# Gate matrices of a mixture of experts in one transfer each, with buffers of their own

## The chip, the core and the metric

One core of a Trainium2 chip runs the whole decoder block in one launch. The metric is the device time of one execution in microseconds. The engines that matter here are TensorE (PE in the profile), VectorE (DVE), ScalarE (ACT), GpSimd (POOL) and SyncE (SP), which computes nothing and issues nearly all transfers, in the order of its program. The core's 16 DMA engines carry them.

## The reference

Sequence 512, width 1024, everything in float32, one layer:

```
h    = rmsnorm(x) ;  proj = h @ w_in                     # pool input, q, k, v, two gates
x    = x + (gate_p * (pool(u) @ w_pool_up) + gate_a * (diff_attention(q, k, v) @ w_attn_up)) @ w_out
hn   = rmsnorm(x)
g    = top-1 of 4 expert groups(hn) ;  e1, e2 = top-2 of the 8 experts in that group
y[t] = sum over e in (e1, e2) of  weight(t, e) * ( (silu(hn[t] @ w_gate[e]) * (hn[t] @ w_up[e])) @ w_down[e] )
out  = x + y
```

There are 32 experts. `w_gate[e]` and `w_up[e]` are 1024 x 512, `w_down[e]` is 512 x 1024: 2 MB each, 192 MB (MiB) in all, and every one is read from HBM in every execution, whichever experts the tokens choose.

## The kernel before

**First part, up to the output projection (some 315 us).** The matrices of the mixer come in 24 pieces of 1 MB (`pieces`). A piece is staged (`stage_to`), then split chunk by chunk by ACT and DVE into a high and a low part in float32r (`split_to`, lines 156 to 160), and PE makes three products for one (`tok_unit`, `ch_unit`). `tick()` stands behind each unit of 12 matmuls and puts the splits of pieces that come later, and other small tasks, between the units. `ch_group(19, ...)` is the last product group ahead of the output projection. Its evacuation (`evac_attn(1)`, lines 562 to 566) makes the second half of the merged branches, `mh` and `ml`. `out_proj()` then multiplies with `w_out`, adds the residual (`acc`), norms, ranks the tokens by expert, and stores the normed rows to DRAM on POOL's queue (`store_rows`), from where later pairs fetch theirs.

**Second part, the experts, two at a time (16 pairs).** A pair has 64 token slots for each of its two experts. Pair p runs in this order on PE: gate product, up product, the rest of the scatter of pair p - 1, transposes of the hidden values (`ht`) and of the next pair's rows (`spread`), down product in two halves (`y`, `half_down`), the scatter of the first half. In the down product, the first half of the columns already uses all four down pieces.

**Buffers.** All large tiles come from one pool of 23 buffers of 8 KB a partition (`S`): x, staged and split pieces, h (two pairs of high and low), attention's o and pooling's y (a pair each), gates, the residual and the normed rows, and then the weights of the experts. A new tile takes the buffer that was given back first; its first writer waits until the old tile's last reader is through. The DMA engines are handed a transfer when SP's wait is over, and whatever SP issues later stands behind it.

**Order of the weights.** `order` lists the pieces of all experts, pair by pair: four of the gates (two halves of two experts, 1 MB each), four of up, four of down. `prefetch(n)` issues the next n of them (line 620). In `out_proj` it is called with 8, 4, 3, 3 and 1; in pair p with 4 behind the gate product, 4 behind the up product (5 for p = 0) and 4 behind the down product. The last pair has smaller pieces: eight of up of 512 KB, two of down of 1 MB, four of down of 512 KB. At the end of `out_proj` one buffer `io` holds x of the current pair in its first half and the rows fetched for the next in its second.

Of the kernel before, what the change touches and what calls it, by code (L numbers as in the profile page):

```python
# [32 lines left out]
NEG = -1.0e30  # L33
W_SCALE = 2.0 ** 14

NBIG = 23
NSM = 8
WARM = 12
LEAD = 6
OUT_ORDER = ((0, 0), (1, 0), (0, 1), (2, 0), (1, 1), (3, 0), (2, 1), (3, 1))  # L40
STG = 2
PF = (8, 4, 3, 3)
PAIR_ORDER = (("g", (0, 1)), ("u", (0, 1)), ("d", (0, 1)))
LAST_ORDER = (("g", (0, 1)), ("v", (0, 1, 2, 3)), ("h", (0,)), ("q", (2, 3)))
PIECE = {"g": (4, 512), "u": (4, 512), "v": (2, 512), "d": (2, 1024), "h": (4, 512), "q": (4, 256)}


@with_exitstack
def hybrid_block_kernel(
# [33 lines left out]
    const = ctx.enter_context(tc.tile_pool(name="const", bufs=1))  # L83
    tiny = ctx.enter_context(tc.tile_pool(name="tiny", bufs=3))
    big = ctx.enter_context(tc.tile_pool(name="big", bufs=NBIG))
    sm = ctx.enter_context(tc.tile_pool(name="sm", bufs=NSM))
    dram = ctx.enter_context(tc.tile_pool(name="dram", bufs=1, space=bass.MemoryType.DRAM))
    psum = ctx.enter_context(tc.tile_pool(name="psum", bufs=8, space=bass.MemoryType.PSUM))
# [3 lines left out]

    def S(shape, dt=F32, name="s"):
        return big.tile(shape, dt, tag="S", name=f"{name}{next(names)}")

    def T(name="t"):
        return sm.tile([128, 512], F32, tag="T", name=f"{name}{next(names)}")
# [4 lines left out]
    def bank(name="b", shape=(128, 512)):  # L102
        return psum.tile(list(shape), F32, tag="B", name=f"{name}{next(names)}")
# [134 lines left out]
        stt(neglam, lsum[:, 1:2], -LAM_INIT, lsum[:, 0:1], op0=OP.add, op1=OP.subtract)  # L238


    hT = [(S([128, 4, SEQ], F32R, name="hTh"), S([128, 4, SEQ], F32R, name="hTl")) for _ in range(2)]
    rst = const.tile([128, NT], F32, name="rst")

    def h_norm(t):
# [70 lines left out]
    def attention():  # L315
# [73 lines left out]

        def o_transpose(i):  # L390
            if i == 0:
                oT.extend((S([128, H, SEQ], F32R, name="oTh"), S([128, H, SEQ], F32R, name="oTl")))
            on = st.pop(("on", i))
            b = bank("to", (128, H, 128))
            for h in range(H):
                nc.tensor.transpose(b[:, h, :], on[:, h * 128:(h + 1) * 128], ident)
            s = slice(i * 128, (i + 1) * 128)
            nc.scalar.mul(oT[0][:, :, s], b, cols[:, 4:5])
            stt(oT[1][:, :, s], b, cols[:, 4:5], f(oT[0][:, :, s]), op0=OP.mult, op1=OP.subtract)
# [20 lines left out]
    def pool_group(g, b):  # L420
        w = POOL_W[g]
        PAD = 16
        z = S([128, 3, PAD + SEQ], name="u")
        nc.gpsimd.memset(z[:, :, :PAD], 0.0)
        u = z[:, 0]
        nc.scalar.copy(u[:, PAD:], b)
        cur, k = 0, 1
        while k < w:
            nxt = 2 if cur == 1 else 1
            nc.gpsimd.tensor_tensor(z[:, nxt, PAD:], z[:, cur, PAD:], z[:, cur, PAD - k:PAD + SEQ - k], op=OP.add)  # L430
            cur, k = nxt, 2 * k
        yield
        s, d = z[:, cur], z[:, 3 - cur, :SEQ]
        stt(d[:, w:SEQ], s[:, PAD + w:], 1.0 / w, u[:, PAD + w:], op0=OP.mult, op1=OP.subtract)
        tt(d[:, :w], s[:, PAD:PAD + w], rc[:, :w], op=OP.mult)
        tt(d[:, :w], d[:, :w], u[:, PAD:PAD + w], op=OP.subtract)
        if g == 0:
            yT.extend((S([128, 4, SEQ], F32R, name="yTh"), S([128, 4, SEQ], F32R, name="yTl")))
        yield
        p = bank("y")  # L440
        mm(p, wgrp[:, g, :], d, start=True, stop=True)
        nc.scalar.mul(yT[0][:, g, :], p, cols[:, g:g + 1])
        stt(yT[1][:, g, :], p, cols[:, g:g + 1], f(yT[0][:, g, :]), op0=OP.mult, op1=OP.subtract)
        yield
# [151 lines left out]
    for e in range(0, NE, 2):  # L596
        for w, parts in LAST_ORDER if e == NE - 2 else PAIR_ORDER:
            for part in parts:
                for par in range(2):
                    order.append((w, e + par, part))  # L600
    e_next = [0]

    def expert_ap(w, e, half):
        e = ds(e, 1) if isinstance(e, int) else e
        if w in "hq":
            n = PIECE[w][1]
            return w_down[e].rearrange("e (p j) n -> p (e j) n", j=4)[:, :, n * half:n * (half + 1)]
        if w == "d":
            return w_down[e].rearrange("e (p j) n -> p (e j) n", j=4)[:, 2 * half:2 * half + 2, :]
        src = w_gate if w == "g" else w_up  # L610
        n = PIECE[w][0]
        return src[e].rearrange("e (p j) n -> p (e j) n", j=8)[:, n * half:n * (half + 1), :]

    def prefetch(n):
        for _ in range(n):
            if e_next[0] < len(order):
                key = order[e_next[0]]
                e_next[0] += 1
                st = S([128, *PIECE[key[0]]], name="e")
                nc.sync.dma_start(st, expert_ap(*key))  # L620
                ew[key] = st
# [21 lines left out]
    tok_row = const.tile([128, SEQ], F32, name="tok_row")  # L643
    nc.gpsimd.iota(tok_row, pattern=[[-1, SEQ]], base=SEQ, channel_multiplier=0, allow_small_or_imprecise_dtypes=True)
    sel = {}
    first = {}

    def x2_half(t, hf, b):
        a = acc_t(t)[:, hf * 512:(hf + 1) * 512]
# [127 lines left out]
    def out_proj():  # L777
        i = N_GEMM
        bs = [bank("wo") for _ in range(NT)]
        prefetch(PF[0])  # L780
        for kq in range(2):
            for t in range(NT):
                tok_unit(bs[t], i + kq, kq, t, merged, kq == 0, kq == 1)
                if kq == 1:
                    x2_half(t, 0, bs[t])
                    after(2, lambda t=t: rt_transpose(t, 0))
                tick()
        prefetch(PF[1])
        last = NT - 1
        bs = {}  # L790
        mid = {}
        for n, (t, kq) in enumerate(OUT_ORDER):
            if kq == 0:
                bs[t] = bank("wo")
            tok_unit(bs[t], i + 2 + kq, kq, t, merged, kq == 0, kq == 1, mid)
            mid = {}
            if kq == 1:
                x2_half(t, 1, bs[t])
                if t == last:
                    rt_select(last - 1, 5)  # L800
                x2_rstd(t)
                if t < last - 1:
                    mid = {1: lambda t=t: rt_transpose(t, 1)}
                    after(2, lambda t=t: norm2(t))
                    after(2, lambda t=t: store_rows(t))
                    after(2, lambda t=t: rt_logits(t, 0, 1))
                    after(2, lambda t=t: rt_select(t))
                    after(3, lambda t=t: ranked(t))
                elif t < last:
                    mid = {0: lambda t=t: rt_transpose(t, 1), 1: lambda t=t: rt_logits(t, 0),  # L810
                           2: lambda t=t: (norm2(t), rt_logits(t, 1), rt_select(t, 3))}
            tick()
        prefetch(PF[2])
        assert not tasks, tasks
        rt_logits(last, 0)
        rt_transpose(last, 1)
        gather_first(0, (0,))
        rt_logits(last, 1)
        rt_select(last - 1)
        ranked(last - 1)  # L820
        norm2(last)
        store_rows(last - 1)
        gather_first(0, (1,))
        gather_first(1)
        rt_select(last)
        prefetch(PF[3])
        first["io"] = S([128, 2, D], name="io")
        gather_first(last - 1)
        ranked(last)
        gather_first(last)  # L830
        store_rows(last)
        prefetch(1)
        pairs[0] = first
        for t in range(NT):
            rt_weights(t)
# [17 lines left out]
            first["x"] = x_of(first["b"])  # L853

    def x_of(bs):
        xT = first["io"][:, 0, :].rearrange("p (j s) -> p j s", j=ND)
        for i, b in enumerate(bs):
            jj = slice(i * 4, (i + 1) * 4)
            tt(xT[:, jj, :], b, g2p[:, jj, None].to_broadcast([128, 4, 128]), op=OP.mult)  # L859
        return xT  # L860
# [7 lines left out]
                                     bounds_check=SEQ - 1, oob_is_err=False)  # L868

    def fetch(p):  # L870
        rows = first["io"][:, 1, :]
        nc.gpsimd.memset(rows, 0.0)  # L872
        fetch_rows(rows, info[p][2])
        pairs[p]["rows"] = rows

# [34 lines left out]
    def ffn_in(b, xs, w, part):  # L910
        n = w[0].shape[1]
        for k in range(n):
            j = part * n + k
            for par in range(len(xs)):
                s = slice(par * CAP, (par + 1) * CAP)
                mm(b[s, :], xs[par][:, j, :], w[par][:, k, :], start=j == 0, stop=j == 7)  # L916
# [67 lines left out]
    def take(w, e, part):  # L984
        return [ew.pop((w, e + par, part)) for par in range(2)]
# [45 lines left out]
    def run_overflow():  # L1031
# [15 lines left out]
        with tc.For_i(0, n_over, 1) as i:  # L1047
# [16 lines left out]
            ts(wv[:CAP, 2:3], wv[:CAP, 0:1], wv[:CAP, 1:2], 1.0 / W_SCALE, op0=OP.add, op1=OP.mult)  # L1064
            for k, b in (("g", banks[3]), ("u", banks[4])):
                for half in range(2):
                    nc.sync.dma_start(w, expert_ap(k, ds(e, 1), half))
                    ffn_in(b, [xT], [w], half)
            nc.scalar.activation(sg[:CAP], banks[3][:CAP], AF.Silu)
            tt(h[:CAP], banks[4][:CAP].rearrange("p (q j) -> p j q", j=4),  # L1070
# [16 lines left out]
    for p in range(n_pair):  # L1087
# [5 lines left out]
            if q < n_pair:  # L1093
                prepare(q)
        bg_ = bank("gate")
        for half in range(2):
            ffn_in(bg_, xs, take("g", e, half), half)
        prefetch(4)
        bu = bank("up")
        for part in LAST_ORDER[1][1] if last_pair else range(2):  # L1100
            ffn_in(bu, xs, take("v" if last_pair else "u", e, part), part)
        prefetch(5 if p == 0 else 4)
        h = ffn_h(bg_, bu, 128)
        adds = [scatter_mms(*prev, t) for t in range(3)] if prev else []
        for q in (0, 1, 2) if p == 0 else (p + 2,):
# [75 lines left out]
```

## Time and profile before

| | |
|---|---|
| median of 3 runs | 800.28 us (798.57 to 801.16) |
| the profiled execution: its time | 800.73 us |
| its span | 798.9 us |
| PE busy | 771.1 us (97%) |
| DVE busy | 361.1 us (45%) |
| ACT busy | 204.0 us (26%) |
| queue of SP and its share of 16 DMA engines | 233.37 MB, 72.5% |
| chain that ended last | PE 70%, DMA 21%, DVE 5% |

All times in views are counted from the start of the span. A busy PE is not PE at its peak: a group of matmuls that waits for data between single matmuls can show as busy. "Idle before" of an engine, and the releaser behind it, say what an engine waited for; for SP's queue the same view lists what its transfers waited for before they were issued.

### The profile page before, as it was taken

The page shows a single profiled execution, that of the slowest core. Times are in us where ns is not written, and L with a number is a line of the kernel's source. Part 1 is how long each engine was busy: PE and PEld are TensorE (multiplying, and loading weights), DVE is VectorE, ACT ScalarE, POOL GpSimd, SP SyncE. Part 2 cuts the span into 40 slices and gives each one's busy share as a digit, 9 for nine tenths or more (in the row PEclk, how much of TensorE's full clock was granted, in tenths as well). Part 3 has the DMA queues.
Part 4 walks back from the last instruction along what each step waited for, and adds up shares of the span by engine and source line. Part 5 has one row for each costly group of instructions (what it writes and reads, how often), then busy time and mean ns, then how long its engine had stood idle before and what let it go on. Part 6 is the DMA issues. An engine that isn't in the chain of part 4 may idle for free.

```text
span 798.9 us, 9648 instructions
## 1 busy us (share of the span) xinstructions
PE 771.1 (97%) x3686; PEld 450.6 (56%) x3686; DVE 361.1 (45%) x848; ACT 204.0 (26%) x390; POOL 69.2 (9%) x85
## 2 busy tenths in 40 slices
PE   7999999999999999999999999999999999999995
PEld 6888777778888888733444344434444333334343
DVE  5644476545464733662536353335343423324233
ACT  5644445554533433420010001000100000001000
POOL 1131060000100001100010000000000000000000
PEclk9999999999999999989999999999999999999998
DMA  9621013113228782989999999999999999999994
GB/s 326 201 81 53 6 48 106 54 53 106 72 89 313 293 340 91 373 353 425 425 427 427 426 426 426 427 425 426 425 427 426 425 427 425 426 427 426 426 397 146
DMA packets 55711, 240.07 MB, mean 301 GB/s; under 512 B 11176, under 2 KB 14760, under 8 KB 32112
## 3 DMA queue, kind: packets, MB, share of 16 engines
q1 hardware_dynamic: 52928, 233.37, 72.5%
q0 software_dynamic: 2736, 6.07, 1.9%
q8 instruction: 30, 0.49, 0.2%
q14 instruction: 17, 0.14, 0.0%
HBM read 239.13 MB, written 4.19 MB: 305 GB/s over the span
## 4 chain that ended last, share of the span: by engine, by line
PE 70%; DMA 21%; DVE 5%; ACT 2%; issue 1%; SPq 0%; POOL 0%; DVEq 0%; ACTq 0%
PE y L965 9%; PE gate L916 8%; PE up L916 8%; DMA e<-in_w_expert_up_dram 8%; DMA e<-in_w_expert_down_dram 7%; PE g L282 6%; PE g L283 6%; PE g L284 6%; DMA e<-in_w_expert_gate_dram 5%; PE sc L977 5%; PE wo L271 2%; PE wo L273 2%; PE wo L272 2%; PE qk L325 1%; PE o L370 1%; PE v L271 1%
## 5 line engine op out<-in xcount | busy, mean ns | idle before, releaser
L916 PE MATMUL up<-e,io 128*64 128x512 f32 x512 | 119.4, 594 | 9.6 <-DMA e<-in_w_expert_up_dram 9.5
L916 PE MATMUL gate<-e,io 128*64 128x512 f32 x512 | 115.4, 596 | 1.7 <-DVE io L859 1.7
L965 PE MATMUL y<-e,hT 128*64 128x512 f32 x480 | 114.1, 605 | 0.7 <-ACT hT L931 0.7
L922 DVE TENSOR_TENSOR h<-up,sg 128x512 f32<-128x512 f32 x16 | 17.2, 1075 | 183.0 <-PE up L916 183.0
L916 PEld LDWEIGHTS up<-e,io 128*64 128x64 f32 x512 | 38.2, 137 | 87.1 <-issue 67.3
L916 PEld LDWEIGHTS gate<-e,io 128*64 128x64 f32 x512 | 37.9, 137 | 69.6 <-issue 60.0
L981 DVE TENSOR_TENSOR acc<-sc,acc 128x512 f32<-128x512 f32 x124 | 76.8, 683 | 0.2
L965 PEld LDWEIGHTS y<-e,hT 128*64 128x64 f32 x480 | 35.4, 139 | 69.0 <-issue 62.8
L157 DVE SCALAR_TENSOR_TENSOR wl<-w,g1c,wh 128x512 fp32r<-128x512 f32 x64 | 49.0, 792 | 38.6 <-ACT wh L156 38.5
L282 PE MATMUL g<-hTh,wh 128*128 128x512 f32 x160 | 64.8, 405 | 0.1
L283 PE MATMUL g<-hTl,wh 128*128 128x512 f32 x160 | 62.4, 390 | 0.0
L284 PE MATMUL g<-hTh,wl 128*128 128x512 f32 x160 | 62.4, 390 | 0.0
L971 DVE SCALAR_TENSOR_TENSOR yl<-y,wv,yh 128x512 fp32r<-128x512 f32 x31 | 23.3, 751 | 76.1 <-ACT yh L970 76.1
L977 PE MATMUL sc<-yh,PT 128*128 128x512 f32 x124 | 53.3, 430 | 0.0
L970 ACT ACTIVATE yh<-y,wv 128x512 fp32r<-128x512 f32 x31 | 21.3, 688 | 118.0 <-PE y L965 113.8
L977 PE MATMUL sc<-yl,PT 128*128 128x512 f32 x124 | 48.9, 394 | 0.0
L931 ACT COPY hT<-ht 128x512 f32<-128x512 f32 x16 | 9.4, 587 | 145.7 <-PE ht L929 145.7
L156 ACT ACTIVATE wh<-w,g1c 128x512 fp32r<-128x512 f32 x64 | 44.6, 720 | 0.9 <-DMA w<-in_w_in_dram 0.9
L872 POOL MEMSET io<- 128x1024 f32 x15 | 14.3, 952 | 335.7 <-PE xg L882 335.7
L920 ACT ACTIVATE sg<-gate 128x512 f32<-128x512 f32 x16 | 9.6, 597 | 130.5 <-PE gate L916 130.5
L977 PEld LDWEIGHTS sc<-yh,PT 128*128 128x128 f32 x124 | 23.3, 188 | 28.1 <-issue 24.7
L282 PEld LDWEIGHTS g<-hTh,wh 128*128 128x128 f32 x160 | 30.0, 188 | 13.1 <-issue 5.4
(227 smaller groups left out, 1089.3 us busy)
## 6 DMA issues: line engine op xcount, KB each, us to landing
e<-in_w_expert_gate_dram SPq DMA_DIRECT2D x64, 1024.0 KB, 19.7
e<-in_w_expert_down_dram SPq DMA_DIRECT2D x62, 1024.0 KB, 19.6
e<-in_w_expert_up_dram SPq DMA_DIRECT2D x60, 1024.0 KB, 20.2
w<-in_w_in_dram SPq DMA_DIRECT2D x16, 1024.0 KB, 5.6
w<-in_w_out_dram SPq DMA_DIRECT2D x4, 1024.0 KB, 6.0
e<-in_w_expert_up_dram SPq DMA_DIRECT2D x8, 512.0 KB, 14.1
x<-in_x_dram SPq DMA_DIRECT2D x4, 512.0 KB, 6.2
w<-in_w_pool_up_dram SPq DMA_DIRECT2D x2, 1024.0 KB, 4.9
```

The costliest lines, as they stand in the source:

```text
L156: nc.scalar.mul(hi, src, g)
L157: stt(lo, src, g, f(hi), op0=OP.mult, op1=OP.subtract)
L271: mm(b, ahi[:, k, s], whi[:, k, :], start=first and k == 0, stop=False)
L282: mm(b, whi[:, k, s], ahi[:, k, :], start=first and k == 0, stop=False)
L283: mm(b, whi[:, k, s], alo[:, k, :], start=False, stop=False)
L284: mm(b, wlo[:, k, s], ahi[:, k, :], start=False, stop=last and k == 3)
L916: mm(b[s, :], xs[par][:, j, :], w[par][:, k, :], start=j == 0, stop=j == 7)
L965: mm(y[r, :], hTt[:, j, r], w[j // 2][par][:, j % 2, hf * 512:(hf + 1) * 512], start=j == 0, stop=j == 3)
L970: nc.scalar.mul(hi, y, wv)
L971: stt(lo, y, wv, f(hi), op0=OP.mult, op1=OP.subtract)
L977: mm(b, PT[:, t * 128:(t + 1) * 128], y2[k], start=k == 0, stop=k == 1)
L981: tt(a, b, a, op=OP.add)
```

## The change

The pool of 23 buffers becomes one of 15 single ones and one of four of double size (16 KB a partition), the same memory. The four hold h (two), y of the pooling and o of attention first, and from the output projection on the gate matrices: one transfer of 2 MB for an expert's whole gate matrix. The list `order` holds up and down only; the gates have an iterator of their own, and `prefetch_gate()` issues the two of a pair. x and the fetched rows get a buffer each, of two halves that take turns; the buffer of the rows is asked for behind the last store of normed rows.

```diff
-NBIG = 23
+NBIG = 15
+NWIDE = 4
-PF = (8, 4, 3, 3)
-PAIR_ORDER = (("g", (0, 1)), ("u", (0, 1)), ("d", (0, 1)))
-LAST_ORDER = (("g", (0, 1)), ("v", (0, 1, 2, 3)), ("h", (0,)), ("q", (2, 3)))
-PIECE = {"g": (4, 512), "u": (4, 512), ...
+PF = (2, 2, 3, 3)
+PAIR_ORDER = (("u", (0, 1)), ("d", (0, 1)))
+LAST_ORDER = (("v", (0, 1, 2, 3)), ("h", (0,)), ("q", (2, 3)))
+PIECE = {"g": (8, 512), "u": (4, 512), ...
+    def split_tile(name):
+        t = wide.tile([128, 2, 4, SEQ], F32R, tag="W", name=f"{name}{next(names)}")
+        return t[:, 0], t[:, 1]
-    hT = [(S([128, 4, SEQ], F32R, name="hTh"), S([128, 4, SEQ], F32R, name="hTl")) for _ in range(2)]
+    hT = [split_tile("hT") for _ in range(2)]
...
+    gates = iter(range(NE))
+    def prefetch_gate():
+        for _ in range(2):
+            e = next(gates, None)
+            if e is not None:
+                st = wide.tile([128, *PIECE["g"]], F32, tag="W", name=f"eg{next(names)}")
+                nc.sync.dma_start(st, expert_ap("g", e, 0))
+                ew["g", e, 0] = st
@@ out_proj
+        prefetch_gate()
         prefetch(PF[0])
+        prefetch_gate()
...
-        first["io"] = S([128, 2, D], name="io")
+        first["xT"] = S([128, 2, D], name="xT")
...
         store_rows(last)
         prefetch(1)
+        first["rows"] = S([128, 2, D], name="rows")
+        nc.gpsimd.memset(first["rows"][:, 1, :], 0.0)
@@ fetch
-        rows = first["io"][:, 1, :]
-        nc.gpsimd.memset(rows, 0.0)
+        rows = first["rows"][:, p % 2, :]
+        if p > 1:
+            nc.gpsimd.memset(rows, 0.0)
@@ loop over pairs
-        for half in range(2):
-            ffn_in(bg_, xs, take("g", e, half), half)
+        ffn_in(bg_, xs, take("g", e, 0), 0)
+        bu = bank("up")
+        for part in LAST_ORDER[0][1] if last_pair else range(2):
+            ffn_in(bu, xs, take("v" if last_pair else "u", e, part), part)
         prefetch(4)
-        bu = bank("up")
-        for part in LAST_ORDER[1][1] if last_pair else range(2):
-            ffn_in(bu, xs, take("v" if last_pair else "u", e, part), part)
-        prefetch(5 if p == 0 else 4)
+        prefetch_gate()
```

The tiles of o and y change as `hT` does, and `x_of` writes the halves of `xT` in turn.

## Rows read from the trace of the kernel before

**Rows 1.** The page's slices of 20 us: granted PE clock in tenths, DMA traffic.
```profile
PEclk9999999999999999989999999999999999999998
GB/s 326 201 81 53 6 48 106 54 53 106 72 89 313 293 340 91 373 353 425 425 427 427 426 426 426 427 425 426 425 427 426 425 427 425 426 427 426 426 397 146
```

**Rows 2.** Stretches: length, busy us per engine (instructions), granted clock, DMA share, GB/s.
```profile
302.00:314.00 12.00, 11.99 (x66) 10.00 (x65) 4.74 (x20) 4.51 (x7) 1.82 (x3) 1.00 0.11 44
339.00:342.50 3.50, 3.50 (x20) 1.18 (x18) 2.41 (x14) 0.88 (x5) 0.00 (x0) 1.00 0.29 119
352.00:358.00 6.00, 4.65 (x14) 1.78 (x16) 2.89 (x13) 0.59 (x1) 1.09 (x1) 0.50 1.00 425
380.00:430.00 50.00, 50.00 (x248) 20.97 (x246) 26.44 (x69) 5.12 (x8) 4.06 (x5) 1.00 1.01 425
700.00:750.00 50.00, 46.29 (x207) 19.75 (x204) 14.63 (x29) 3.68 (x6) 1.95 (x2) 1.00 1.01 427
```

**Rows 3.** Chain of waits from 710 on: start, us, what (engine or transfer).
```profile
733.92 19.56 DMA e<-in_w_expert_down_dram
753.52 5.36 PE y L965 x22
...
760.93 7.02 PE gate L916 x32
767.95 7.31 PE up L916 x31
```

**Rows 4.** SP's issues from 729 to 747: start, us to the last one's end, count.
```profile
728.70 5.55 SPq L620 DMA_DIRECT2D e<-in_w_expert_down_dram  x3
736.41 7.65 SPq L620 DMA_DIRECT2D e<-in_w_expert_gate_dram  x4
```

**Rows 5.** SP's issues after the pause, from 300 to 362.
```profile
314.79 10.32 SPq L620 DMA_DIRECT2D e<-in_w_expert_gate_dram  x4
325.16 6.26 SPq L620 DMA_DIRECT2D e<-in_w_expert_up_dram  x3
...
331.09 10.95 SPq L620 DMA_DIRECT2D e<-in_w_expert_up_dram  x2
342.14 2.25 SPq L620 DMA_DIRECT2D e<-in_w_expert_down_dram  x4
```

**Rows 6.** What SP's queue waited for: us in total, times, longest.
```profile
SPq L620 <- DMA xn_rows<-xn: 10.1, 1, 10.1
```

**Rows 7.** PE in pair 0 and at pair 1's up product: start, us.
```profile
335.56 7.09 PE L916 MATMUL gate<-e,io 128*64 128x512 f32 x32
342.47 7.04 PE L916 MATMUL up<-e,io 128*64 128x512 f32 x32
...
354.46 9.07 PE L965 MATMUL y<-e,hT 128*64 128x512 f32 x32 [0.68 <-ACT hT L931]
...
375.04 7.04 PE L916 MATMUL up<-e,io 128*64 128x512 f32 x32
```

**Rows 8.** DMA in 500 to 550, then in 751 to 764: packets, sizes, queue 1.
```profile
DMA packets 3051, 21.30 MB, mean 426 GB/s; under 512 B 421, under 2 KB 421, under 8 KB 484
q1 hardware_dynamic: 2886, 21.01, 99.6%
...
DMA packets 979, 5.41 MB, mean 416 GB/s; under 512 B 108, under 2 KB 108, under 8 KB 531
q1 hardware_dynamic: 978, 5.39, 100.0%
```

**Rows 9.** DVE in the last product group before the output projection.
```profile
265.88 0.69 DVE L566 TENSOR_TENSOR ml<-m,mh 128x512 fp32r<-128x512 f32 x1 [0.69 <-ACT mh L565]
266.49 0.68 DVE L160 TENSOR_TENSOR wl<-w,wh 128x512 fp32r<-128x512 f32 x1
...
269.80 0.69 DVE L160 TENSOR_TENSOR wl<-w,wh 128x512 fp32r<-128x512 f32 x1
```

**Rows 10.** PE's first matmul of the output projection.
```profile
271.73 0.39 PE L271 MATMUL wo<-wh,mh 128*128 128x512 f32 x1
```

More of the change, by code (lines that the diff above doesn't have):

```diff
@@ L41 @@
 STG = 2
-PF = (8, 4, 3, 3)
-PAIR_ORDER = (("g", (0, 1)), ("u", (0, 1)), ("d", (0, 1)))
-LAST_ORDER = (("g", (0, 1)), ("v", (0, 1, 2, 3)), ("h", (0,)), ("q", (2, 3)))
-PIECE = {"g": (4, 512), "u": (4, 512), "v": (2, 512), "d": (2, 1024), "h": (4, 512), "q": (4, 256)}
+PF = (2, 2, 3, 3)
+PAIR_ORDER = (("u", (0, 1)), ("d", (0, 1)))
+LAST_ORDER = (("v", (0, 1, 2, 3)), ("h", (0,)), ("q", (2, 3)))
+PIECE = {"g": (8, 512), "u": (4, 512), "v": (2, 512), "d": (2, 1024), "h": (4, 512), "q": (4, 256)}
 @with_exitstack
@@ L85, in hybrid_block_kernel @@
     big = ctx.enter_context(tc.tile_pool(name="big", bufs=NBIG))
+    wide = ctx.enter_context(tc.tile_pool(name="wide", bufs=NWIDE))
     sm = ctx.enter_context(tc.tile_pool(name="sm", bufs=NSM))
@@ L391, in o_transpose @@
             if i == 0:
-                oT.extend((S([128, H, SEQ], F32R, name="oTh"), S([128, H, SEQ], F32R, name="oTl")))
+                oT.extend(split_tile("oT"))
             on = st.pop(("on", i))
@@ L437, in pool_group @@
         if g == 0:
-            yT.extend((S([128, 4, SEQ], F32R, name="yTh"), S([128, 4, SEQ], F32R, name="yTl")))
+            yT.extend(split_tile("yT"))
         yield
@@ L601, in hybrid_block_kernel, with expert_ap @@
     e_next = [0]
-    def expert_ap(w, e, half):
+    gates = iter(range(NE))
[6 more added lines that the diff above has]
+                ew["g", e, 0] = st
+    def expert_ap(w, e, half, n=None):
         e = ds(e, 1) if isinstance(e, int) else e
@@ L610, in expert_ap @@
         src = w_gate if w == "g" else w_up
-        n = PIECE[w][0]
+        n = PIECE[w][0] if n is None else n
         return src[e].rearrange("e (p j) n -> p (e j) n", j=8)[:, n * half:n * (half + 1), :]
@@ L645, in hybrid_block_kernel @@
     sel = {}
-    first = {}
+    first = {"n": 0}
     def x2_half(t, hf, b):
@@ L855, in x_of @@
     def x_of(bs):
-        xT = first["io"][:, 0, :].rearrange("p (j s) -> p j s", j=ND)
+        xT = first["xT"][:, first["n"] % 2, :].rearrange("p (j s) -> p j s", j=ND)
+        first["n"] += 1
         for i, b in enumerate(bs):
@@ L1066, in run_overflow @@
                 for half in range(2):
-                    nc.sync.dma_start(w, expert_ap(k, ds(e, 1), half))
+                    nc.sync.dma_start(w, expert_ap(k, ds(e, 1), half, 4))
                     ffn_in(b, [xT], [w], half)
```

## The prediction

> **What bounds the kernel now.** I read the 40 slices first, then a table of stretches, then the end of the chain of waits, then SP's own queue. The slices [rows 1] show two parts: up to some 240 us little traffic, from 360 us a flat 425 to 427 GB/s to the end. The table by stretch [rows 2] says what the flat part is: in 380 to 430 TensorE (PE) is busy all 50.00 us and the DMA engines are full as well; in 700 to 750 DMA is still full and PE is busy 46.29 of 50 us. So the weight stream never stops, PE runs ahead on what was loaded early until that lead is used up, and then it waits for the stream. The chain [rows 3] shows the last wait: the last quarter of pair 14's down weights is issued at 733.92, lands 19.56 us later, and at 753.52 PE goes on with y; from there the chain stays on PE through the gate product of the last pair (760.93), its up product (767.95) and on to the end. The end is therefore fixed by one landing: 798.9 - 753.5 = 45.4 us of work follow it, nearly all PE in program order. Whatever moves that landing moves the time, one for one.
>
> Other prices used below: 1 MB (1.049e6 bytes) takes 1.049 / 0.427 = 2.46 us of the stream, 12 MB of a pair and 0.5 MB of its gathered rows 30.7 us.
>
> **The change, part by part.** The profiled run took 800.73 us for a span of 798.9; I make the sum on these and take 0.45 off at the end, since the median of the runs is 800.28.
>
> *Place of the gates in the queue.* In the kernel before, one list orders all weights, so pair 14's four down quarters go out in a row and the four gate pieces of pair 15 behind them [rows 4]. In the changed one SP issues, behind each up product, four single pieces and then the two gate transfers of the pair after next. Count the singles: 2 + 2 + 3 + 3 + 1 = 11 ahead of the loop, then 8 a pair, so behind the up product of pair p the single pieces issued are 11 + 8p + 4. For p = 13 that is 119, and 119 is the third of pair 14's four down quarters (singles 117 to 120). The 4 MB of gate 15 come next and the fourth quarter only behind them. SP is one queue in order and DMA is full, so that quarter lands 4 x 2.46 = 9.8 us later: **+9.8 us**. PE cannot use the gates earlier: its program has y of pair 14 first. What follows the landing stays at 45.4 us: the last pair's up pieces, 4 MB, land within 9.8 us of it, while rest of y, scatter and gate keep PE 767.95 - 753.52 = 14.4 us [rows 3]; the later pieces, 4 MB more, have 10 us beyond that.
>
> *Restart after routing.* DMA stands nearly still from 302 to 314 because buffers are full [rows 2]; it goes on when the output projection gives buffers back, 7 pieces issued from 314.79 to 331.09 [rows 5]. The next piece is issued 10.95 - 0.33 = 10.6 us later, at 341.7; 10.1 us of that is the wait for the store of the normed rows, whose buffer it takes [rows 6]. The stream runs dry meanwhile: 119 GB/s in 339 to 342.5 [rows 2]. In the changed kernel the fetched rows get that buffer. Fifteen singles are 2 for the residual, 1 for x, 1 for the rows and 11 for weights, all handed out by then, so single number 12 must wait for a quarter of pair 0's up weights. PE gives the first back at half of the up product: 342.47 + 3.52 = 346.0 [rows 7]. The gate buffers of pair 0 are free from 342.5, but their refill stands behind four singles in the same queue. 19 pieces' worth of weights are loaded at both restarts, so the stream is later by 346.0 - 341.7: **+4.3 us**. The three singles behind it go at 346.0 and 349.5, so the stream holds: four singles, two gates, four singles, 12 MB in all from 347.0 to some 377.8. The next single needs a quarter of pair 1's up weights, free at 375.04 + 3.5 = 378.6 [rows 7], with data a microsecond later: a second hole, **+1.8 us**. From pair 2 on the buffer is free before the stream needs it. Bounds for both holes together: 3.5 us (traffic is low until 342.5 now, and the second hole does not show) to 9.6 us (the first buffer comes only with the end of the up product, at 349.5, and the second hole shows).
>
> *Fewer, larger packets.* A gate transfer moves 16 KB rows in place of 8 KB. The trace has no 16 KB packet. In 500 to 550, 2886 packets of queue 1 fill 99.6% of 16 engines; without the small ones that is 310 ns per 8 KB packet; in 751 to 764 with 423 packets of 4 KB among them the same division leaves some 162 ns for 4 KB [rows 8]. So 4 KB cost 148 ns and a packet some 13 ns by itself. A pair's gates are 32 packets of 8 KB on each engine; 16 fewer save 0.2 us a pair, for 14 pairs 2.9 us. Bounds: 0 (rows go out in 8 KB pieces as now) to -2.9; I take **-2.0**, nearer to the row.
>
> *Buffers ahead of the loop.* The four double buffers start as h (two), y of the pooling and o of attention, eight former singles. Their number is the same, but singles can no longer use what the pooled y frees before the loop. In the last product group before the output projection 16 singles are wanted at once: two gates, merged half 0 (hi, lo), the split pieces 19 and 20 (4), four staged pieces, two residual buffers, merged half 1 (hi, lo). So DVE's first write of the last one, at 265.88 [rows 9], has to wait until piece 19 is through, which is when PE goes over to the output projection at 271.73 [rows 10]. Queued behind it on DVE are the two remaining splits of piece 20 (266.49 and 269.80 now), the second of them behind another block's chain of 3.3 us: it would end at some 276.7. PE wants it at 274.0, as the fourth k (3 x 0.68 us and one matmul behind 271.73) of its first unit: **+2.7 us**, and all that follows is later by this. Bounds: 0 (the hand-out gives the late buffer to a residual load, which has 25 us to spare) and 6.0 (the whole of DVE's wait).
>
> *The rest.* Two buffers for x and for the rows take away waits of GpSimd that nobody is behind: the fetched rows are wanted a pair later. If that cover went, a fetch would cost what DMA takes for it, 1.2 us. Waiting for a whole gate transfer instead of half a one costs nothing, since the gates come before the quarter that PE waits for.
>
> Sum: 9.8 + 4.3 + 1.8 - 2.0 + 2.7 = 16.6 us; 800.73 + 16.6 - 0.45 = **817 us**.
>
> **Rivals.**
> 1. *The gates' place costs nothing, the holes alone count.* It would be so if PE had a lead at the last quarter. For it: in 380 to 430 the lead is there, PE waits for nothing. Against it: 753.52 follows directly on the landing, and PE is idle 7% in 700 to 750 [rows 2, 3]. Time: 800.3 + 4.3 + 1.8 - 2.0 + 2.7 = 807.
> 2. *The clock falls in the gathered wait.* Now PE's idle time is spread over several short waits a pair, and the granted clock stays at 1.00 in 700 to 750; in the changed kernel it stands at one place, ahead of the last down quarter, some 3 us. In pair 0 the clock did fall behind a stretch of small products, to 0.50 in 352 to 358, the lower of its two levels (1.2 GHz for 2.4), and y took 9.07 us there [rows 2, 7] where the gate product of as many matmuls took 7.09. Before the last pairs the stream hides that; after the last landing it is paid, 2 us by that row, and up to 3 if all of the 6 us at half clock are full of matmuls: 817 + 3 = 820. The Trainium skill, "TensorE: Matmul & The Clock Gate", in its part on a loop that waits for DMA at every weight tile, says that such waits put the clock back to half each time; this trace shows a fall in pair 0 (0.50), but behind small products, and none for the short waits of 700 to 750 (1.00).
> 3. *Faster: two pools act as two streams.* If the buffers, not SP's program, set the order, the refill of the gates starts when pair 0's gates are through (342.5), the freed queue no longer stands 10.1 us behind the store, the 3.5 us of low traffic close, and each down quarter goes ahead of the next gates. Then, with DVE's wait at its lower bound, -3 - 2.0 us: 795. It decides at the first refill: are the gate transfers issued before or after the singles of the up product? Against it: one wait at SP holds everything behind it now (four pieces go out in 2.25 us as soon as the 10.95 us are over, [rows 5]).
>
> **How the numbers follow.** Forecast 0.62 (own range 811 to 821, by the bounds of packets, holes and the DVE wait); rival 1 0.12; rival 2 0.16; rival 3 0.05; 0.05 for something that evens the holes out. What a measurement of this kernel can tell from no change is about 0.3%. Slower: 0.62 + 0.12 + 0.16 = 0.90; faster 0.05; same 0.05. The range reaches from rival 1 to beyond rival 2: 805 to 823, with about 0.15 outside.
>
> **What would show it.** In the changed trace: SP's queue has the two gate transfers of pair 15 ahead of one lone down piece; the chain's last DMA link is that piece, landing near 770, with 45 us behind it; DMA has a hole of some 8 us between 340 and 352 and a short one near 380; the packets of 16 KB take just over 600 ns; DVE has a stop of up to 6 us near 266 and PE a gap under 3 us near 274. PE waits once a pair, inside y, when its lead is used up. The prediction is wrong if y of pair 14 does not wait for its last quarter, or if that quarter lands before 760.

## The result and the profile after

| | before | after |
|---|---|---|
| median | 800.39 us (798.57 to 801.16, with the runs beside after) | 819.43 us (818.59 to 822.63), 4 runs |
| the profiled execution: its time, its span | 800.73, 798.9 us | 819.56, 817.8 us |
| mean granted clock | 0.991 | 0.978 |
| chain that ended last: PE, DMA | 70%, 21% | 63%, 28% |

The ratio is 1.0244 [1.0228, 1.0261]: slower by 19 us, 2.4 more than forecast and inside the range.

The page's slices, as [rows 1]:

```profile
PEclk9999999999999999989999999999999899899998
GB/s 319 148 25 103 52 52 103 84 20 131 76 103 255 276 343 164 299 355 376 427 430 423 430 431 421 429 430 424 428 432 422 427 431 425 426 431 425 414 246 105
```

The stream of weights reaches the same plateau as before, but a slice later, and the granted clock dips in two slices (near 640 and 705 us) in which it did not in [rows 1]. The table by stretch says where the stream begins late (columns as in [rows 2]):

```profile
339.00:342.50 3.50, 3.50 (x18) 1.22 (x20) 2.47 (x12) 0.88 (x5) 0.00 (x0) 1.00 1.03 427
342.50:350.00 7.50, 7.50 (x38) 2.47 (x36) 5.28 (x28) 1.81 (x11) 0.99 (x1) 1.00 0.11 47
380.00:430.00 50.00, 50.00 (x250) 20.91 (x248) 23.03 (x59) 4.52 (x7) 4.03 (x5) 1.00 0.99 410
381.00:384.00 3.00, 3.00 (x16) 1.01 (x14) 0.00 (x0) 0.00 (x0) 0.00 (x0) 1.00 0.57 167
700.00:750.00 50.00, 45.05 (x202) 19.70 (x200) 19.50 (x40) 4.53 (x7) 2.96 (x3) 0.93 1.01 426
```

The 3.5 us of low traffic before 342.5 are closed. In their place stand a first hole (7.5 us with 47 GB/s) and a second one at 381 to 384, in which the DMA engines are idle for 43% of the time, 1.3 us. PE is busy in all of it: the holes cost nothing where they are. The end of the chain of waits, as [rows 3]:

```profile
747.54 24.38 DMA e<-in_w_expert_down_dram
771.96 6.79 PE y L987 x22
778.75 2.04 PE sc L999 x8
780.79 7.02 PE gate L938 x32
787.81 6.87 PE up L938 x32
```

The same link ends it as before, a down quarter that lands, now at 771.92 instead of 753.48: +18.4 us. Behind it are 45.9 us (45.4 before). That the quarter is the one forecast is seen in SP's queue. Before, the fourth quarter followed the other three and the gates came behind it [rows 3, 4]; now the two gate transfers stand between the third and the fourth:

```profile
732.71 6.56 SPq L636 DMA_DIRECT2D e<-in_w_expert_down_dram  x3
741.38 3.24 SPq L616 DMA_DIRECT2D eg<-in_w_expert_gate_dram  x2
747.54 0.33 SPq L636 DMA_DIRECT2D e<-in_w_expert_down_dram  x1
750.04 5.18 SPq L636 DMA_DIRECT2D e<-in_w_expert_up_dram  x3
```

And the queue at the restart, where [rows 5] had one pause, from 331.5 to 341.7:

```profile
328.51 21.26 SPq L636 DMA_DIRECT2D e<-in_w_expert_up_dram  x4
349.87 3.82 SPq L636 DMA_DIRECT2D e<-in_w_expert_down_dram  x3
353.74 1.03 SPq L616 DMA_DIRECT2D eg<-in_w_expert_gate_dram  x2
365.43 0.33 SPq L636 DMA_DIRECT2D e<-in_w_expert_down_dram  x1
365.86 16.73 SPq L636 DMA_DIRECT2D e<-in_w_expert_up_dram  x4
382.68 3.81 SPq L636 DMA_DIRECT2D e<-in_w_expert_down_dram  x3
```

The last of the first four up pieces goes out near 349.5, halfway through pair 0's up product (345.82 to 352.86), and nothing behind it can go earlier: neither the gates of pair 2, whose buffers are free from the end of pair 0's gate product at 346.0, nor anything else. The same happens with the last of the next four, near 382.3.

Ahead of all this, PE reaches pair 0's gate product at 338.90 instead of 335.56. DVE's and PE's rows (as [rows 9, 10]) show why:

```profile
272.56 0.69 DVE L573 TENSOR_TENSOR ml<-m,mh 128x512 fp32r<-128x512 f32 x1 [6.59 <-PE g L290]
```

```profile
274.34 0.40 PE L280 MATMUL wo<-wh,ml 128*128 128x512 f32 x1
276.40 0.49 PE L278 MATMUL wo<-wh,mh 128*128 128x512 f32 x1 [1.66 <-ACT wh L166]
277.21 0.50 PE L279 MATMUL wo<-wl,mh 128*128 128x512 f32 x1 [0.31 <-DVE wl L167]
```

DVE stands still for 6.59 us ahead of the second merged half, and PE then waits for the split of the fourth k. In the profiled executions of all the kernels here (e1 to e8 are the experiments below), PE takes the same time from its first product of the output projection to pair 0's gate product as long as DVE does not stop there: 63.8 us in before, e3, e5, e7 and e8. With the stop it takes 66.4 in after, e2 and e2b. In e1 and e6 it takes 68.0, because there the granted clock also falls right behind the stop (0.89 from 270 to 285, 1.00 in after).

**The stream's lateness in one number.** Packets of 4 KB and more carry the weights. The table gives the end of the packet with which 60 and 180 MB (of 2^20 bytes) of them have passed in each profiled execution, as lateness against before (429.2 and 724.6 us); "PE" is the lateness of pair 0's gate product (335.56 before). The fifth column is 800.73 plus the lateness at 180 MB, plus 9.9 for the order of the queue (measured in e5 below) where the gates still go ahead of the last down quarter.

| kernel (edits below) | PE | at 60 MB | at 180 MB | 800.73 + stream + order | its time |
|---|---|---|---|---|---|
| after | 3.3 | 9.7 | 8.9 | 819.5 | 819.56 |
| e1, down ahead of the gates | 4.3 | 10.9 | 10.1 | 810.8 | 812.18 |
| e2, gates first in pair 0 | 2.4 | 8.4 | 7.5 | 818.2 | 816.82 |
| e2b, gates first in pairs 0, 1 | 2.7 | 5.2 | 4.4 | 815.0 | 813.84 |
| e3, residual late | -0.2 | 6.7 | 5.8 | 816.4 | 815.14 |
| e5, before with gates ahead | 0.2 | 0.0 | 0.0 | 810.6 | 809.75 |
| e6, gates in halves | 4.5 | 10.5 | 10.4 | 821.0 | 819.99 |
| e7, mended | 3.1 | 3.4 | 2.7 | 803.4 | 805.38 |
| e8, mended, halves | 2.5 | 3.0 | 2.9 | 803.6 | 804.64 |

Two terms, how late the stream is and whether the gates go ahead, give every profiled time within 2.0 us, over a spread of 15. The 3.1 and 2.5 us of PE in e7 and e8 do not come from the edits: in these two executions PE was late by as much when it reached the output projection (274.79 and 274.25; 271.73 in before), ahead of all that they edit, behind a stretch of half clock near 13 us that before did not have. First before, then e7:

```profile
0.00:20.00 20.00, 15.46 (x79) 12.77 (x80) 10.39 (x20) 11.36 (x20) 3.93 (x13) 1.00 0.93 326
```

```profile
0.00:20.00 20.00, 14.69 (x62) 11.88 (x63) 9.78 (x19) 11.18 (x19) 3.93 (x13) 0.83 0.91 321
```

Set against that, their streams at 180 MB stand where before's does (-0.4 and +0.4).

### The profile page after: what moved, and what is told of

Its sections match the earlier page's. It is cut to its first block, busy times and chain, and to the rows that moved or that the text cites. A ratio compares the mean times of both kernels' runs of the same rounds, so it can differ in the third digit from the quotient of the medians.

```text
span 817.8 us, 9558 instructions
## 1 busy us (share of the span) xinstructions
PE 776.9 (95%) x3686; PEld 450.2 (55%) x3686; DVE 362.2 (44%) x848; ACT 204.0 (25%) x390; POOL 69.5 (8%) x85
## 4 chain that ended last, share of the span: by engine, by line
PE 63%; DMA 28%; DVE 5%; ACT 2%; issue 1%; SPq 0%; POOL 0%; DVEq 0%; ACTq 0%
DMA e<-in_w_expert_down_dram 18%; PE y L987 10%; DMA e<-in_w_expert_up_dram 9%; PE gate L938 6%; PE g L289 6%; PE g L290 6%; PE g L291 6%; PE up L938 5%; PE sc L999 4%; PE wo L278 2%; PE wo L279 2%; PE wo L280 2%; PE qk L332 1%; DMA w<-in_w_in_dram 1%; PE o L377 1%; PE v L278 1%
## 5 line engine op out<-in xcount | busy, mean ns | idle before, releaser
L987 PE MATMUL y<-e,hT 128*64 128x512 f32 x480 | 127.0, 649 | 20.3 <-DMA e<-in_w_expert_down_dram 19.5
L938 PE MATMUL gate<-eg,xT 128*64 128x512 f32 x512 | 113.4, 595 | 1.7 <-DVE xT L880 1.7
L938 PE MATMUL up<-e,xT 128*64 128x512 f32 x512 | 112.6, 592 | 0.0
L987 PEld LDWEIGHTS y<-e,hT 128*64 128x64 f32 x480 | 39.3, 148 | 97.5 <-issue 69.3
L944 DVE TENSOR_TENSOR h<-up,sg 128x512 f32<-128x512 f32 x16 | 17.1, 1070 | 166.6 <-PE up L938 166.6
L938 PEld LDWEIGHTS up<-e,xT 128*64 128x64 f32 x512 | 36.8, 137 | 73.1 <-issue 73.1
L938 PEld LDWEIGHTS gate<-eg,xT 128*64 128x64 f32 x512 | 35.3, 137 | 70.7 <-issue 63.7
L289 PE MATMUL g<-hT,wh 128*128 128x512 f32 x160 | 64.9, 405 | 0.1
L291 PE MATMUL g<-hT,wl 128*128 128x512 f32 x160 | 62.4, 390 | 0.0
L290 PE MATMUL g<-hT,wh 128*128 128x512 f32 x160 | 62.4, 390 | 0.0
L888 POOL DMA_INDIRECT rows<-xn_rows,idx x15 | 15.1, 1007 | 356.4 <-DVE idx L885 356.1
L163 ACT ACTIVATE wh<-w,g1c 128x512 fp32r<-128x512 f32 x64 | 44.6, 720 | 1.8 <-DMA w<-in_w_in_dram 1.8
L289 PEld LDWEIGHTS g<-hT,wh 128*128 128x128 f32 x160 | 30.0, 188 | 13.1 <-issue 5.4
```

Of the source, the lines that this page charges most:

```text
L163: nc.scalar.mul(hi, src, g)
L289: mm(b, whi[:, k, s], ahi[:, k, :], start=first and k == 0, stop=False)
L290: mm(b, whi[:, k, s], alo[:, k, :], start=False, stop=False)
L291: mm(b, wlo[:, k, s], ahi[:, k, :], start=False, stop=last and k == 3)
L987: mm(y[r, :], hTt[:, j, r], w[j // 2][par][:, j % 2, hf * 512:(hf + 1) * 512], start=j == 0, stop=j == 3)
```

## The experiments

**The order, undone in the changed kernel (e1).** From pair 2 to pair 13 a fifth single goes out behind the up product, so that the four down quarters stay together and the gates follow.

```diff
-        prefetch(4)
+        ahead = 1 if 2 <= p < n_pair - 2 else 0
+        prefetch(4 + ahead)
         prefetch_gate()
...
-        prefetch(4)
+        prefetch(4 - ahead)
```

> The changed kernel, with one single piece more behind the up product and one less behind the down product in pairs 2 to 13, so that the last down quarter of a pair goes out ahead of the 4 MB of gates. Theory (place in the queue, +9.8 us, and the clock's fall in the wait that it gathers, 1.4 us of y in pair 14): that quarter of pair 14 lands near 762 and the time is 819.4 - 9.8 - 1.4 = 808 us (806 to 811), the granted clock stays at 1.00 past 400 us. Rival (the place costs nothing, only the holes of the restart count): 819 us.

Measured: 810.67 (810.07 to 812.18), ratio to before 1.0127 [1.0107, 1.0146]. So 8.8 us of the 19 go with the order alone. y of pair 14 waits no more; the wait moves to the gate product of the last pair, whose 4 MB now land behind the quarter and are needed whole:

```profile
748.69 24.44 DMA eg<-in_w_expert_gate_dram
773.13 0.04 issue
773.18 6.65 PE gate L938 x29
```

That the granted clock would stay at 1.00 past 400 us did not come true: it fell behind the waits for whole gates near 591, 683 and 745 us.

**The order, made in the kernel before (e5).** Nothing but the list is changed: the gates of each pair from pair 2 on stand ahead of the last down quarter of the pair before.

```diff
+    for e in range(4, NE, 2):
+        at = order.index(("g", e, 0))
+        order[at - 1:at + 4] = order[at:at + 4] + order[at - 1:at]
```

> The kernel before, with its one pool of 23, all buffers and all sizes as they were; only its list of weights is reordered from pair 2 on: the four gate pieces of a pair go ahead of the last down quarter of the pair before. Theory (the place in the queue alone): the last quarter of pair 14 lands 9.8 us later, at some 763.5, and y waits for it in one gathered wait behind which the clock falls: 800.5 + 9.8 + 1.4 = 811 us (809 to 813.5). Rival (the place costs only together with the two pools or the fewer buffers): 800 to 803 us.

Measured: 809.4 (807.8 to 811.68), 1.0109 [1.0079, 1.0139]. The stream is not late at all (0.0 in the table), and yet the landing moves from 753.48 to 763.42, +9.94 us:

```profile
743.85 19.57 DMA e<-in_w_expert_down_dram
763.41 0.04 issue
763.46 5.37 PE y L968 x22
```

That is the place of the gates in the queue by itself, without a new buffer or a larger transfer. The span grows by less, 9.1 us: 44.6 us follow the landing instead of 45.4, since the last pair's up and down products no longer wait for their pieces (6.87 for 7.31 us [rows 3], and 9.3 for 9.7). And y stayed at full clock, where a fall of the clock had been expected to cost 1.4 us.

**The holes (e2, e2b).** The gates go ahead of the four singles behind pair 0's up product (e2), or behind those of pairs 0 and 1 (e2b), so that the queue's head is a transfer whose buffer is free.

```diff
+        if p == 0:          # e2b: p < 2
+            prefetch_gate()
         prefetch(4)
-        prefetch_gate()
+        if p > 0:           # e2b: p > 1
+            prefetch_gate()
```

> The changed kernel, with the gates of pair 2 issued ahead of the four singles in pair 0. They wait for the gate buffers of pair 0 only (free near 346 us, for 349.45), so the first hole is 3.4 us shorter. Theory A (each hole counts by itself): 819.4 - 3.4 = 816.0 us. Theory B (the second hole, at 383 us, waits for PE's up product of pair 1 whatever came before, so it grows by what the first one loses): 819.4 us, unchanged, with the hole near 383 us at some 5 us.

> The same in pairs 0 and 1, so that the gates of pair 3 (buffers free near 379 us) bridge the second hole. Theory B: now the 3.4 us and the 1.8 us of the second hole both come back, 819.4 - 5.2 = 814.2 us (812.5 to 816). Rival (an early lead of the stream is worth nothing in the end): 819.4 us.

Measured: e2 819.07 (816.82 to 819.37), 1.0231 [1.0214, 1.0249]; e2b 813.84 (812.67 to 815.34), 1.0170 [1.0151, 1.0189]. Traffic at the two holes, first e2, then e2b:

```profile
342.50:350.00 7.50, 7.50 (x37) 2.44 (x34) 5.08 (x25) 2.15 (x13) 0.95 (x1) 1.00 0.54 192
378.00:390.00 12.00, 12.00 (x66) 5.42 (x64) 4.94 (x11) 0.71 (x2) 1.97 (x2) 1.00 0.67 264
```

```profile
342.50:350.00 7.50, 7.50 (x38) 2.56 (x36) 4.87 (x24) 2.23 (x15) 0.95 (x1) 1.00 0.53 183
378.00:390.00 12.00, 12.00 (x64) 5.41 (x62) 4.93 (x11) 0.76 (x2) 1.97 (x2) 1.00 0.96 386
```

In after the first stretch has 47 GB/s, and the second is:

```profile
378.00:390.00 12.00, 12.00 (x64) 5.41 (x62) 3.62 (x9) 1.19 (x2) 1.50 (x2) 1.00 0.90 350
```

e2 closes a good part of the first hole and gets next to nothing for it: what came earlier fills the buffers earlier, and the stream stands longer at the second one. Set against PE's own lateness, the stream at 60 MB is 6.4 us late in after (9.7 - 3.3), 6.0 in e2 and 2.5 in e2b. So the first of the two theories (each hole counts for itself) falls; only with both gone is there a gain.

**The wait of DVE (e3).** The last product group is issued ahead of the two residual loads, so that these, not the merged half, take the late buffers.

```diff
+    ch_group(19, [oT], evac_attn(1))
     acc = [S([128, 2, D], name="acc") for _ in range(2)]
...
         nc.sync.dma_start(acc[t], x_rows[t * 256:(t + 1) * 256, :].rearrange("(t p) d -> p t d", p=128))
-    ch_group(19, [oT], evac_attn(1))
```

> The changed kernel, with the two residual buffers asked for and loaded behind the last product group, so that DVE's first write of the merged half finds a free buffer. Theory (DVE's wait of 6.6 us at 266 us stops PE for 1.66 + 0.31 us and what belongs to it, 2.6 us in all, and shifts the rest): the PE gap near 275 us is gone and the time is 819.4 - 2.6 = 816.8 us; that the first 12 MB of weights start 10 us later is hidden, since the stream stands still from 304 to 318 us. Rival (the start of the stream counts): 819.4 - 2.6 + up to 10, slower than the changed kernel.

Measured: 815.65 (814.09 to 816.33), 1.0189 [1.0171, 1.0208], 3.8 us less than after, where 2.6 were expected. PE's gap near 275 is gone, pair 0's gate product is back at its place, and the stream is 3.1 us earlier at 180 MB:

```profile
335.32 6.23 PE L938 MATMUL gate<-eg,xT 128*64 128x512 f32 x28
```

Of the 4.4 us between the two profiled executions 3.0 lie ahead of the landing of pair 14's last quarter. The other 1.4 lie behind it, where the clock falls in after and not in e3.

**Size of the transfers (e6).** The changed kernel with each gate matrix in two transfers of 1 MB, 8 KB rows, into the same buffers.

```diff
-        nc.sync.dma_start(st, expert_ap("g", e, 0))
+        for half in range(2):
+            nc.sync.dma_start(st[:, 4 * half:4 * half + 4, :], expert_ap("g", e, half, 4))
```

> The changed kernel, its gates in the same double buffers and at the same place, but each in two transfers of 1 MB with rows of 8 KB. Theory (the larger transfer is worth its packets, 611 ns for one of 16 KB against twice 309.5, 16 a pair and engine, 14 pairs): 819.4 + 1.7 = 821 us. Rival (the larger transfer itself costs, by its coarser landing): below 818 us. Third (neither): 819.4 us.

Measured: 819.7 (817.92 to 821.45), 1.0236 [1.0211, 1.0261]. The time can't tell 1.7 us from nothing here. The stream can: from 60 to 180 MB it makes up 0.8 us on before in after and 0.1 in e6. The other traces say the same: 0.7 to 0.9 us in all six kernels with gates of 2 MB, 0.1 in the two with halves. So the large transfers with their 16 KB packets are worth 0.7 us in 120 MB, ten pairs.

**Both mended (e7, e8).** e7 takes e3 and e2b's order (with one single ahead of the gates in pair 0), and lets the fetched rows share x's buffer again, so that one single more is left for weights. Pair 0 issues that piece more, and from there on a pair's four down quarters stay together ahead of the next gates. Gates stay 2 MB. e8 is e7 with the gates in halves, first halves of both experts first. Of e7's edit this is the part that e3 has not, in short form:

```diff
-        rows = first["rows"][:, p % 2, :]
+        rows = first["io"][:, 1, :]      # x of the pair: first["io"][:, 0, :]
...
+        if p == 0:
+            prefetch(1)
+        if p < 2:
+            prefetch_gate()
         prefetch(4)
-        prefetch_gate()
+        if p > 1:
+            prefetch_gate()
```

> The changed kernel with its four prices taken back and the 2 MB gates and four double buffers kept: x and fetched rows share one single buffer again (12 singles for weights, so the last down quarter is ahead of the gates), the residual buffers behind the last product group, gates ahead of the other pieces in pairs 0 and 1. Theory: the stream is where it was in the kernel before, less 1.7 us of packets, but the gate product must wait for all 4 MB, as the first experiment showed, some 2.5 us: 801 us (799 to 803). Rival (two pools cost something else that is not among the four): 805 us and more.

> The same with the gates in 1 MB halves, first halves of both experts first, so that the gate product can start on them. Theory (what is left in the run before is the landing of whole gates, 2.5 us, against 1.7 us of packets): 800.2 us (798.5 to 802), and no wait of PE ahead of the gate product. Rival (whole landings cost nothing): 801 + 1.7 = 802.7 us.

Measured, 12 runs each: e7 801.52, 1.0008 [0.9994, 1.0022]; e8 800.84, 1.0005 [0.9992, 1.0018]. Neither can be told from before, and none is faster. Their profiled executions were the longest of the 12 (805.38, 804.64), late from 13 us on, as said above. The chains differ, first e7, then e8:

```profile
741.93 24.45 DMA eg<-in_w_expert_gate_dram
766.38 0.04 issue
766.43 6.65 PE gate L934 x29
```

```profile
738.00 19.58 DMA e<-in_w_expert_down_dram
757.58 0.04 issue
757.62 5.36 PE y L984 x22
```

In e7 PE waits for a whole 2 MB gate matrix, and the granted clock falls three times (at 614, 675 and 737); in e8, with halves, it waits for the down quarter as before did, and the clock stays at 1.00 from 361 to 797.

## Why the prediction was right, step by step

- **What sets the end: right.** A landing of a down quarter of pair 14, then 45.9 us of work. Every version with the gates ahead ends like this; in e2 and e3 the quarter lands within 0.2 us of PE's arrival (below).
- **Place of the gates, +9.8: right.** SP's queue is as counted (three quarters, gates, one quarter); e5 gives +9.94 at the landing and +9.1 in the span, e1 gives back 8.8. What e1 doesn't give back of the 9.9 is the next wait, for the whole of the last gates, which the prediction had not looked for.
- **What follows the landing, 45.4: right by luck.** It measured 45.9. Two things that the forecast had at nothing nearly cancel: the waits inside before's last pair are gone (44.6 in e5, 44.4 in e6, where the clock stays), and the fall of the clock in y costs 1.4.
- **Two holes, 4.3 + 1.8: right in sum, wrong in kind.** The stream loses 6.4 behind PE's own lateness for the 6.1 forecast, at the places forecast. But the two are not separate costs, as their sum makes them look: e2 shows that closing the first widens the second. What is paid in all is set by the second, where the singles run out again.
- **DVE's wait, +2.7: right.** 6.59 us at DVE; two PE gaps of 1.97 us together, and 2.6 us of lateness at pair 0's gate product beyond the 0.8 by which this execution reached the output projection later (272.51 for 271.73). The four other executions with the stop lose as much or, with the clock's fall, 1.6 more; the five without it lose nothing. e3 gives back 3.8 us of time, 1.4 of it behind the landing.
- **Packets, -2.0: half of that.** The packets of 500 to 550, as [rows 8]:

```profile
DMA packets 2685, 21.44 MB, mean 429 GB/s; under 512 B 433, under 2 KB 433, under 8 KB 505
q1 hardware_dynamic: 2448, 21.10, 99.6%
```

  There a 16 KB packet takes 611 ns and one of 8 KB 309.5, so that one in place of two saves 8 ns (13 forecast, from the stretch with 4 KB packets), and the stream kept 0.7 us of ten pairs, half of the 1.3 that 8 ns make there; an estimate for fourteen is 1.0. The Trainium skill, "DMA: Bandwidth & Descriptors", section on measured bandwidth, gives 341 GB/s for a transfer of 1 MB and 425 for 16 MB, and the rule to batch to at least 1 MiB. The kernel before keeps that rule, and its 1 MB transfers, queued one behind the other, ran at 425 to 427 already [rows 1, 2]: the 341 does not hold for such a queue, and larger transfers had next to nothing left to give.
- **Waiting for whole gate transfers, 0: right here, not in general.** In after the wait is for the quarter behind them. Once the order is mended they are what PE waits for (e1, e7), and halves move the wait back to the quarter (e8).
- **Rival 1 (holes alone): fell** by e5. **Rival 3 (two streams): fell** by the SP rows: the gates of pair 2, with buffers free from 346.0, go out only at 353.74, behind the waiting up piece and three down pieces.
- **Rival 2 (the clock falls in the gathered wait): came true in part.** PE's line for y on the page:

```profile
L987 PE MATMUL y<-e,hT 128*64 128x512 f32 x480 | 127.0, 649 | 20.3 <-DMA e<-in_w_expert_down_dram 19.5
L938 PE MATMUL up<-e,xT 128*64 128x512 f32 x512 | 112.6, 592 | 0.0
```

  With the waits ahead of y, idle gaps of 3.1 to 5.0 us, the granted clock fell to 0.50, from 2.4 to 1.2 GHz, five times, for 3.4 or 6.8 us. At the last of them the 22 matmuls of y took 6.79 us for 5.36: 1.4 us, where rival 2 had 2 to 3. The Trainium skill, "TensorE: Matmul & The Clock Gate", section on oscillation, has a loop that waits 3 to 5 us for DMA at every weight tile start every tile at the lower clock. The traces agree in part: with the last gap 3.33 us long in e5 and in e6, y took 5.37 and 5.36 at full clock. In e6:

```profile
773.88 5.36 PE L988 MATMUL y<-e,hT 128*64 128x512 f32 x22 [3.33 <-DMA e<-in_w_expert_down_dram]
```
- **"Once a pair": right in place, not in size.** The large waits in after lie 60 us apart (they begin at 526, 586, 646, 707 and 769), in every second pair. In the pairs between, the quarter lands within 0.9 us of PE's arrival, or just ahead of it. Part of this rhythm can be read off y's first product with the last quarter: at full clock PE is back there after 26.8 to 26.9 us, and after 28.4 to 29.5 where the clock fell, so that the fall takes from the next wait what it costs. Also, the next quarter comes 29.3 to 29.5 us behind a large wait and 30.5 to 32.3 behind a small one; why that alternates I did not settle. In the profiled executions of e2 and e3 the large waits fall on the other pairs, the last one ending at 741 and 739 us, and the chain names PE from there on. But pair 14's last quarter lands at 770.59 and 768.90, and y goes on with it at 770.64 and 768.95, 0.2 and 0.1 us after PE could have. So the landing still sets the end there, 17.1 and 15.4 us later than before's, for 17.4 and 15.7 by the table's two terms.

The sum of what was measured: 9.9 (order) + 3.3 (PE later, 0.8 of it this execution's) + 6.4 (holes) - 0.8 (packets, to 180 MB) = 18.8, for a landing 18.4 later; 0.5 more behind it make the span's 18.9. The forecast's 16.6 lacked the 0.8, took 1.2 too much for packets up to there, and had the 0.5 behind the landing at nothing. The other terms were off by 0.3 or less.

## What to carry to other kernels

With one queue in order, the two pools of buffers here did not make two streams: the first transfer without a buffer held all behind it (gates with free buffers from 346.0 to 353.7), and closing one such hole was worth 0.4 us of the stream while the next still stood. Before grouping transfers, count which piece the last wait needs, and what is now issued ahead of it: here each MB cost its 2.5 us there in full (e5: 9.94 us for 4 MB). To price such a change, measure the stream's lateness at a fixed number of bytes and the order at its end as two terms.

## What was not expected of the hardware

- PE's waits of nearly the same length did and did not cost the clock. In after it fell with gaps of 3.11, 3.17 and 3.52 us, in e7 already at one of 2.33; in e3 it stayed at 1.00 behind 3.11 and 3.26, in e5 and e6 behind 3.33 us. Behind the waits of 1.2 us that lie ahead of the up product in before and e8 it never fell. What decides between them is open.
- A gate matrix as one transfer of 16 KB rows moves per byte 1.3% faster than in 8 KB rows (611 ns for 619), on a third of the weights alone, and the stream kept half of that gain.
